# Spreading the operations with sums over a pair of column blocks, and more steps before a turned block is copied, in a hybrid decoder layer on Trainium2

## The chip, the cores and the metric

One core of one Trainium2 chip runs the whole layer. The metric is the device time in microseconds (us); the kernel before was run three times.

## The reference, cut to what matters

The reference is one decoder layer over x of 256 tokens by 2048 features, all in float32:

```
h = rmsnorm(x);  proj = h @ w_in                      # 2048 -> 16400 columns
hm = sigmoid(mo) * head_rmsnorm(mlstm(mq, mk, mv))    # 8 heads
hd = head_rmsnorm(diff_attention(dq, dk, dv))         # 8 heads
y  = sigmoid(gm) * (hm @ w_bm) + sigmoid(gd) * (hd @ w_bd)
x  = x + y @ w_out
h  = rmsnorm(x)
x  = x + (silu(h @ w_gate) * (h @ w_up)) @ w_down     # 2048 -> 5632 -> 2048
out = rmsnorm(x)
```

## The kernel before, in words

**Products.** Each matrix product is cut into column blocks of 512. A `Product` multiplies 256 tokens by one block: 16 steps (`kt`), each with six matmuls (two token halves, and three terms, because activations and weights are each split in a high and a low fp32r part). ScalarE casts the high part of the weights (`wh`, L460 in a `Product`, L313 in a `Pair`), VectorE subtracts it for the low part (`wl`, L461 and L317). One such split covers two steps, is called four units ahead of the matmuls (`AHEAD = 4`), and goes into one of five buffers, so the split for unit u+4 can start when unit u-1 has left TensorE. Raw weights arrive in 1 MB loads on SyncE's queue into `N_RAW = 4` buffers.

**Pairs.** In the feed-forward part a `Pair` multiplies one group of input chunks (512 features each) by two column blocks at once: gate and up (`fgu0` to `fgu10`), or two blocks of the down projection (`fd00`, `fd02`, `fd10`, `fd12`, `fd20`). Its first chunk is multiplied in seven operations instead of eight, with sums of blocks (table `SEVEN`): call them s0 to s6. s3 to s6 need a sum of two weight blocks first, an addition on VectorE in place (`sum_up`, L305). Each seven takes 6 matmuls and writes one PSUM bank. The other chunks are plain operations, p0 to p11 for three of them (four to a chunk), each with 12 matmuls into two banks. `Pair.plan` sets the order: one seven, one plain, in turn, and the plain ones that are left at the end: s0 p0 s1 p1 ... s6 p6 p7 ... p11. `fd20` has three chunks, so s0 to s6 and p0 to p7. Eight banks P1 to P8 hold a pair; `quarters` reads them on VectorE (L392) two ticks after each is finished, and the result of a gate-and-up pair is a block `g`.

**Side work.** All other work is written as generators that are resumed by `side.tick()`, so that their instructions stand between those of the products in each engine's program order. A `Product` ticks once a step, a `Pair` once after a seven and twice in a plain one: in both cases once for six matmuls. `yield n` skips n ticks, a bare `yield` none. Generators in one lane run one after the other; the lane `tr` has the transposed copies of y, x1 and g. Where a product needs a chunk whose copy isn't issued yet, `side.until` ticks on the spot until it is.

**Turned blocks.** A block of 256 tokens by 512 features becomes the left operand of the next product when it is transposed. For the kinds named in `TURN` this is `turn_task` (L231): two transposes of 32x32 squares on VectorE (`turned`, L237), one DMA out to DRAM from GpSimd's queue (L242), four DMAs back into `across` (L247), and then, on ScalarE and VectorE, the high and the low part (L260 and L261; with a scale by column first L264, then L265 and L266):

```python
yield 1
...
yield TURN_OUT
t = c4([P, 4, 4 * TT, 32], "across")
for b in range(4):
    nc.gpsimd.dma_start(...)
yield TURN_BACK
hi, lo = dst.alloc(g)
```

With `TURN_OUT, TURN_BACK = 4, 4` the DMA out is issued at the task's 5th tick, the DMAs back at its 10th, the two halves of the copy at its 15th and 16th, and it ends at the 17th (18th where sums are added, `add_up`). GpSimd has no other work there, so it does not wait for ticks: it issues the DMAs back when the DMA out has landed. The kinds not in `TURN` (the last block of y is one) are transposed on TensorE through PSUM (`ps_tr`, L192). An existing helper `turn` (L221) transposes a block without any DMA, in 16 operations on VectorE of 32 partitions each (L227); the convolution's first inputs use it.

**Order around the change.** Products `bd0` to `bd3`, then `wo0` to `wo3`, then `fgu0` to `fgu3`, `fd00`, `fd02`, `fgu4` to `fgu7`, `fd10`, `fd12`, `fgu8` to `fgu10`, `fd20`, and the last two blocks. `bd_done` pushes a block of y, `wo_done` one of x1, and `gate_up_post` one of g, each into lane `tr`. `across_task` chooses the way of transposing.

Of the kernel before, what the change touches and what calls it, by code (L numbers as in the profile page):

```python
# [9 lines left out]
F32 = mybir.dt.float32  # L10
F32R = mybir.dt.float32r
I32 = mybir.dt.int32
AF = mybir.ActivationFunctionType
ALU = mybir.AluOpType
AX = mybir.AxisListType

P = 128
S = 256
# [18 lines left out]
N_T2 = 9  # L37
N_RAW = 4
AHEAD = 4
TURN_OUT, TURN_BACK = 4, 4  # L40
ORDER = (
    "mq0 mk0 mo0 mo1 mv0 mv1 mq1 mk1 mo2 mo3 mv2 mv3 gm0 gm1 gm2 gm3 bm0 bm1 bm2 bm3 "
    "dq0 dk0 dv0 dq1 dk1 dv1 dq2 dk2 dv2 dq3 dk3 dv3 gd0 gd1 gd2 gd3 bd0 bd1 bd2 bd3"
)
N_WARM = (6, 2)
TURN = {"q0", "k0", "hm1", "hm2", "hm3", "dq", "dk", "hd3", "y", "x1", "x1last", "g", "glast4"}


@with_exitstack
def hybrid_block(ctx, tc, x, attn_norm_w, w_in, conv_w, conv_b, b_igate, b_fgate, mlstm_norm_w,  # L50
# [4 lines left out]
    nc = tc.nc  # L55
# [16 lines left out]
    def c4(shape, name, dt=F32):  # L72
        return c4p.tile(shape, dt, tag="c4", name=name)
# [8 lines left out]
    def t2(shape, name, dt=F32):  # L82
        return smp.tile(shape, dt, tag="t2", name=name, bufs=N_T2)
# [51 lines left out]
    side = Side()  # L135
# [69 lines left out]
                                               in1=hi[:, k].bitcast(F32), op0=ALU.mult, op1=ALU.subtract)  # L205

    def across_task(kind, tile, dst, g, scale_col=None, rate=2):
        if kind in TURN:
            yield from turn_task(tile, dst, g, scale_col, rate)
        else:  # L210
            yield from transpose_task(lambda tt, j: tile[:, tt, j * P:(j + 1) * P], dst, g, scale_col)

    def transpose_task(src, dst, g, scale_col=None):
        yield 2
        dst.alloc(g)
        transpose_half(src, dst, g, 0, scale_col)
        yield 2
        transpose_half(src, dst, g, 1, scale_col)
        dst.ready[g] = True

    def turn(src, t, rate=2):  # L221

        for n in range(16):
            a, b = n // 4, n % 4
            i = src[32 * a:32 * a + 32].rearrange("p t (k q f) -> p t k q f", q=4, f=32)[:, :, :, b]
            o = t[32 * b:32 * b + 32].rearrange("p k (t q s) -> p t k q s", q=4, s=32)[:, :, :, a]
            nc.vector.transpose(out=o, in_=i)  # L227
            if n % rate == rate - 1:
                yield

    def turn_task(src, dst, g, scale_col=None, rate=2):  # L231

# [90 lines left out]
    class Pair:  # L323
# [9 lines left out]
        def plan(self, feed):  # L333
            keys, sevens, plain = {}, [], []
            for ch in self.chunks:
                if ch in self.sums:
                    for i, (bank_, (blk, h), add, x) in enumerate(SEVEN):
                        frees = [(ch, 1)] if i == 5 else [(ch, 0)] if i == 6 else []
                        sevens.append((ch, (ch, blk), h, add and ((ch, add[0]), add[1]), [(bank_, x)], frees))
                else:  # L340
                    for blk in range(2):
                        for h in range(2):
                            uses = [((("P1", "P7"), ("P2", "P8"))[blk][t], (t, h)) for t in range(TT)]
                            plain.append((ch, (ch, blk), h, None, uses, [(ch, blk)] if h else []))
            order = []
            while sevens or plain:
                order += [sevens.pop(0)] if sevens else []
                order += [plain.pop(0)] if plain else []
            self.ops = []
            for ch, raw, h, add, uses, frees in order:  # L350
                if raw not in keys:
                    keys[raw] = len(feed.groups)
                    feed.groups.append((self, raw))
                self.ops.append(Op(self, ch, keys[raw], h, add and (keys[add[0]], add[1]), uses,
                                   [keys[f] for f in frees]))
            feed.units += self.ops
            names = [b for op in self.ops for b, _ in op.uses]
            self.left = {b: 2 * names.count(b) for b in names}
# [30 lines left out]
    def quarters(pair):  # L389

        def op(o, i0, i1, op_):
            nc.vector.tensor_tensor(out=o, in0=i0, in1=i1, op=op_)  # L392
        ps = pair.banks
        yield from pair.after("P3", 2)
        s3, u, v, x = (t2([P, 512], f"q{i}") for i in range(4))
        nc.scalar.copy(out=s3, in_=ps["P3"])
        yield from pair.after("P6", 2)
        op(u, s3, ps["P6"], ALU.subtract)
        op(v, u, ps["P4"], ALU.add)
        yield  # L400
        op(x, v, ps["P5"], ALU.subtract)
        op(u, ps["P5"], u, ALU.subtract)
        for t, c, b, o, op_ in ((0, 0, "P1", s3, ALU.add), (1, 0, "P7", v, ALU.subtract),
                                (0, 1, "P2", u, ALU.add), (1, 1, "P8", x, ALU.add)):
            yield from pair.after(b, 2)
            op(o, ps[b], o, op_)
            yield t, c, o
# [190 lines left out]
    def warm_up(n):  # L598

        wps = accp.tile([P, 512], F32, tag="acc", name="ps_warm")  # L600
        for _ in range(n):
            nc.tensor.matmul(wps[:, 0:P], lhsT=wz, rhs=wz, start=True, stop=True)
# [21 lines left out]
    def start_hook(kt):  # L624
        def f():
            c, j = kt // 4, kt % 4
            if kt < 2:
                xt_half(0, kt, 1)
                if kt == 0:
                    warm_up(N_WARM[1])  # L630
            if c < 3 and j >= 2:
# [133 lines left out]
    def conv_task(tok, ft0, dst):  # L765
# [3 lines left out]
        dst.alloc(0)  # L769
        if dst.name in TURN:  # L770
            t = c4([P, 4, S], "turned")
            yield from turn(tok, t)
        for pr in range(2):
            y = t2([P, 2, S], "cv")
            if dst.name in TURN:
                ps = t[:, 2 * pr:2 * pr + 2]
# [85 lines left out]
    def mlstm_group(g, q, k, va):  # L862
        while not (gt and q.ready[0] and k.ready[0]):
            yield
        hraw = c4([P, TT, 2, DV], "hraw")
        ssq = small([P, 4], "ssq")
        ts = []
        for j in range(2):
            ts.append(side.spawn(mlstm_head(2 * g + j, 2 * (g % 2) + j, q, k, va, j, hraw, ssq)))
            yield 3  # L870
        while not (all(t[2] for t in ts) and g in so):
            yield
        yield 1
        rs = norm_pair(ssq, "m")
        yield 1
        for tt in range(TT):
            for j in range(2):
                nc.vector.scalar_tensor_tensor(out=hraw[:, tt, j], in0=hraw[:, tt, j],
                                               scalar=rs[:, 2 * tt + j:2 * tt + j + 1],
                                               in1=so[g][:, tt, j * DV:(j + 1) * DV],  # L880
                                               op0=ALU.mult, op1=ALU.mult)
            yield
        del so[g]
        yield 2
        side.push("across", across_task(f"hm{g}", hraw.rearrange("p t h d -> p t (h d)"), hmT, g, mn_col, 1 if g < 2 else 2))
# [126 lines left out]
    def diff_group(g, q, k, dv):  # L1012
        while not (q.ready[0] and k.ready[0]):
            yield
        hd = c4([P, TT, 2, DV], "hd")
        ssq = small([P, 4], "ssq")
        ts = []
        for j in range(2):
            ts.append(side.spawn(diff_head(j, q, k, dv, hd, ssq)))
            yield 2  # L1020
        while not all(t[2] for t in ts):
            yield
        yield 1
        rs = norm_pair(ssq, "d", 1.0 - LAM_INIT)
        yield 1
        for tt in range(TT):
            for j in range(2):
                nc.vector.tensor_scalar(out=hd[:, tt, j], in0=hd[:, tt, j],
                                        scalar1=rs[:, 2 * tt + j:2 * tt + j + 1], scalar2=None, op0=ALU.mult)
        yield 2  # L1030
        side.push("across", across_task(f"hd{g}", hd.rearrange("p t h d -> p t (h d)"), hdT, g, dn_col))

    def feat_done(side_name):
        def f(acc):
            tok = tokens_of(acc, "dqk")
            dst = Split(1, f"d{side_name}")
            qk[side_name] = dst
            side.push("conv", across_task("d" + side_name, tok, dst, 0, rate=2))
        return f
# [50 lines left out]
    def gate_up_post(gT, i):  # L1090
        def task(pair):
            g = c4([P, TT, 512], "g")
            for got in quarters(pair):
                if got is None:
                    yield
                    continue
                t, c, q = got
                if c == 0:
                    nc.scalar.activation(out=g[:, t], in_=q, func=AF.Silu, scale=r2(t))
                else:  # L1100
                    nc.vector.scalar_tensor_tensor(out=g[:, t], in0=q, scalar=r2(t), in1=g[:, t],
                                                   op0=ALU.mult, op1=ALU.mult)
            side.push("tr", across_task("g", g, gT, i))
        return task

    ss2 = small([P, TT, 4], "ss2", bufs=1)
# [105 lines left out]
    for pi, (f0, f1) in enumerate(parts):  # L1212
        gT = Split(f1 - f0, f"gT{pi}", {0})
# [14 lines left out]

    warm_up(N_WARM[0])

# [66 lines left out]
```

## Time and profile before

| what | us |
|---|---|
| median of three runs | 1810.53 |
| lowest and highest run | 1809.64, 1811.13 |
| the profiled execution, its own time | 1814.74 |
| its span, from the first to the last instruction | 1813.0 |
| TensorE (PE) busy in it | 1746.1 |
| VectorE (DVE) busy | 1262.7 |
| ScalarE (ACT) busy | 911.8 |
| GpSimd (POOL) busy | 88.8 |

Rows are read so: line of the kernel, engine, operation, output tile, inputs, count, then times; "idle before" or "waited for" is time in which the engine had nothing to do, and the name behind it is what ended that wait. A number in the name of an accumulator is left out by the profile, so all pairs of one kind have one name.

### The profile page before, as it was taken

The page shows a single profiled execution, that of the slowest core. Times are in us where ns is not written, and L with a number is a line of the kernel's source. Part 1 is how long each engine was busy: PE and PEld are TensorE (multiplying, and loading weights), DVE is VectorE, ACT ScalarE, POOL GpSimd, SP SyncE. Part 2 cuts the span into 40 slices and gives each one's busy share as a digit, 9 for nine tenths or more (in the row PEclk, how much of TensorE's full clock was granted, in tenths as well). Part 3 has the DMA queues.
Part 4 walks back from the last instruction along what each step waited for, and adds up shares of the span by engine and source line. Part 5 has one row for each costly group of instructions (what it writes and reads, how often), then busy time and mean ns, then how long its engine had stood idle before and what let it go on. Part 6 is the DMA issues. An engine that isn't in the chain of part 4 may idle for free.

```text
span 1813.0 us, 20500 instructions
## 1 busy us (share of the span) xinstructions
PE 1746.1 (96%) x7769; PEld 1432.9 (79%) x7769; DVE 1262.7 (70%) x1678; ACT 911.8 (50%) x1187; POOL 88.8 (5%) x181
## 2 busy tenths in 40 slices
PE   9999999999999999999999998999998999998968
PEld 7888888888888888888888776777886777886756
DVE  6776866655466766764666686777887778886766
ACT  6555655553445555554445554444444444444433
POOL 1000000000010010000101000000000000000000
PEclk9999999999999999999999999999999999999989
DMA  9656575665686676757776565666556666555652
GB/s 306 199 170 186 165 205 169 199 222 191 201 235 189 202 221 197 201 175 219 258 242 221 174 212 183 209 209 209 186 186 203 194 206 209 200 195 186 217 177 93
DMA packets 179955, 363.57 MB, mean 201 GB/s; under 512 B 9984, under 2 KB 11664, under 8 KB 179856
## 3 DMA queue, kind: packets, MB, share of 16 engines
q1 hardware_dynamic: 169744, 330.78, 57.6%
q0 software_dynamic: 10080, 31.47, 5.8%
q8 instruction: 61, 1.00, 0.2%
q14 instruction: 38, 0.31, 0.0%
q10 hardware_dynamic: 32, 0.01, 0.0%
HBM read 344.40 MB, written 17.83 MB: 200 GB/s over the span
## 4 chain that ended last, share of the span: by engine, by line
PE 75%; DVE 8%; DMA 7%; issue 7%; ACT 2%; POOL 1%; ACTq 0%; DVEq 0%; POOLq 0%
DMA across<-across 5%; PE acc_fgu_P L180 3%; PE acc_fgu_P L181 3%; PE acc_fgu_P L179 3%; DVE wl_fgu L317 3%; PE acc_fd_P L180 3%; PE acc_fd_P L179 3%; PE acc_fd_P L181 3%; DMA across<-turned 2%; PE acc_mv L179 2%; PE acc_mo L179 2%; PE acc_dq L179 2%; PE acc_gm L179 2%; PE acc_dk L179 2%; PE acc_gd L179 2%
## 5 line engine op out<-in xcount | busy, mean ns | idle before, releaser
L313 ACT CAST wh_fgu<-wr_fgu 128x1024 fp32r<-128x1024 f32 x209 | 212.0, 1048 | 170.7 <-DVE wr_fgu L305 96.7
L317 DVE TENSOR_TENSOR wl_fgu<-wr_fgu,wh_fgu 128x1024 fp32r<-128x1024 f32 x209 | 250.7, 1219 | 52.9 <-ACT wh_fgu L313 49.9
L180 PE MATMUL acc_fgu_P<-wl_fgu,x1Th 128*128 128x512 f32 x594 | 237.9, 401 | 18.6 <-DVE wl_fgu L317 18.6
L179 PE MATMUL acc_fgu_P<-wh_fgu,x1Th 128*128 128x512 f32 x594 | 236.9, 399 | 18.8 <-ACT wh_fgu L313 17.8
L181 PE MATMUL acc_fgu_P<-wh_fgu,x1Tl 128*128 128x512 f32 x594 | 235.5, 396 | 0.0
L180 PEld LDWEIGHTS acc_fgu_P<-wl_fgu,x1Th 128*128 128x128 f32 x594 | 114.2, 192 | 49.0 <-DVE wl_fgu L317 25.5
L179 PEld LDWEIGHTS acc_fgu_P<-wh_fgu,x1Th 128*128 128x128 f32 x594 | 114.1, 192 | 47.8 <-ACT wh_fgu L313 22.5
L313 ACT CAST wh_fd<-wr_fd 128x1024 fp32r<-128x1024 f32 x91 | 92.3, 1048 | 85.2 <-DVE wr_fd L305 44.2
L181 PEld LDWEIGHTS acc_fgu_P<-wh_fgu,x1Tl 128*128 128x128 f32 x594 | 114.3, 192 | 23.5
L317 DVE TENSOR_TENSOR wl_fd<-wr_fd,wh_fd 128x1024 fp32r<-128x1024 f32 x91 | 108.6, 1219 | 16.6 <-ACT wh_fd L313 15.3
L242 POOL DMA_DIRECT2D across<-turned x30 | 16.9, 565 | 1459.2 <-DVE turned L237 1459.2
L247 POOL DMA_DIRECT2D across<-across x120 | 65.4, 552 | 170.2 <-DMA across<-turned 71.1
L461 DVE TENSOR_TENSOR wl_bm<-wr_bm,wh_bm 128x1024 fp32r<-128x1024 f32 x32 | 39.1, 1225 | 40.6 <-ACT wh_bm L460 40.6
L461 DVE TENSOR_TENSOR wl_bd<-wr_bd,wh_bd 128x1024 fp32r<-128x1024 f32 x32 | 39.1, 1224 | 33.4 <-ACT wh_bd L460 33.4
L461 DVE TENSOR_TENSOR wl_dv<-wr_dv,wh_dv 128x1024 fp32r<-128x1024 f32 x32 | 38.9, 1219 | 33.2 <-ACT wh_dv L460 33.2
L461 DVE TENSOR_TENSOR wl_gm<-wr_gm,wh_gm 128x1024 fp32r<-128x1024 f32 x32 | 39.1, 1223 | 27.9 <-ACT wh_gm L460 27.7
L461 DVE TENSOR_TENSOR wl_gd<-wr_gd,wh_gd 128x1024 fp32r<-128x1024 f32 x32 | 39.0, 1223 | 27.6 <-ACT wh_gd L460 27.4
L460 ACT CAST wh_bd<-wr_bd 128x1024 fp32r<-128x1024 f32 x32 | 33.7, 1055 | 48.3 <-PE acc_bd L181 40.6
L460 ACT CAST wh_bm<-wr_bm 128x1024 fp32r<-128x1024 f32 x32 | 33.6, 1054 | 47.9 <-PE acc_bm L181 41.1
L461 DVE TENSOR_TENSOR wl_dq<-wr_dq,wh_dq 128x1024 fp32r<-128x1024 f32 x32 | 39.2, 1224 | 26.5 <-ACT wh_dq L460 26.0
L461 DVE TENSOR_TENSOR wl_wo<-wr_wo,wh_wo 128x1024 fp32r<-128x1024 f32 x32 | 38.8, 1220 | 26.2 <-ACT wh_wo L460 26.2
L461 DVE TENSOR_TENSOR wl_mv<-wr_mv,wh_mv 128x1024 fp32r<-128x1024 f32 x32 | 38.9, 1221 | 23.1 <-ACT wh_mv L460 22.9
(426 smaller groups left out, 4624.7 us busy)
## 6 DMA issues: line engine op xcount, KB each, us to landing
wr_fgu<-in_w_ffn_gate_dram SPq DMA_DIRECT2D x44, 1024.0 KB, 7.6
wr_fgu<-in_w_ffn_up_dram SPq DMA_DIRECT2D x44, 1024.0 KB, 5.8
wr_fd<-in_w_ffn_down_dram SPq DMA_DIRECT2D x44, 1024.0 KB, 6.0
wr_mo<-in_w_in_dram SPq DMA_DIRECT2D x16, 1024.0 KB, 5.5
wr_mv<-in_w_in_dram SPq DMA_DIRECT2D x16, 1024.0 KB, 5.4
wr_gm<-in_w_in_dram SPq DMA_DIRECT2D x16, 1024.0 KB, 5.6
wr_bm<-in_w_branch_m_dram SPq DMA_DIRECT2D x16, 1024.0 KB, 5.1
wr_dq<-in_w_in_dram SPq DMA_DIRECT2D x16, 1024.0 KB, 5.4
```

The costliest lines, as they stand in the source:

```text
L179: nc.tensor.matmul(o, lhsT=a[0], rhs=b[0], start=first, stop=False)
L180: nc.tensor.matmul(o, lhsT=a[0], rhs=b[1], start=False, stop=False)
L181: nc.tensor.matmul(o, lhsT=a[1], rhs=b[0], start=False, stop=last)
L242: nc.gpsimd.dma_start(out=d.rearrange("a f b n -> (a f) (b n)"), in_=y.rearrange("p b k t s -> p (b k t s)"))
L247: nc.gpsimd.dma_start(out=t[32 * b:32 * b + 32].rearrange("p a u s -> p a (u s)"), in_=d[:, :, b].rearrange("a f n -> f a n"))
L313: nc.scalar.copy(out=hi, in_=r)
L317: nc.vector.tensor_tensor(out=lo, in0=r, in1=hi.bitcast(F32), op=ALU.subtract)
L460: nc.scalar.copy(out=hi[:, i:i + step], in_=r)
L461: nc.vector.tensor_tensor(out=lo[:, i:i + step], in0=r, in1=hi[:, i:i + step].bitcast(F32), op=ALU.subtract)
```

## The change

The order of a pair's operations is no longer alternate: sevens and plain ones are sorted by their relative place, (i + 0.5) / count. For 7 and 12 this gives p0 s0 p1 p2 s1 p3 s2 p4 p5 s3 p6 p7 s4 p8 s5 p9 p10 s6 p11, for 7 and 8 p0 s0 p1 s1 ... p6 s6 p7. `TURN_BACK` goes from 4 to 10, for all that use `turn_task`. The last block of the feed-forward part (`g` of `fgu10`, now kind `glast`) is turned by `turn_short_task`: 16 transposes on VectorE, four to a tick, then the two halves of the copy; no DMA and no trip to DRAM.

```diff
-TURN_OUT, TURN_BACK = 4, 4
+TURN_OUT, TURN_BACK = 4, 10
...
+SHORT = {"glast"}
...
     def across_task(kind, tile, dst, g, scale_col=None, rate=2):
-        if kind in TURN:
+        if kind in SHORT:
+            yield from turn_short_task(tile, dst, g, scale_col, rate)
+        elif kind in TURN:
...
+    def turn_short_task(src, dst, g, scale_col=None, rate=2):
+        yield 1
+        t = c4([P, 4, S], "turned")
+        yield from turn(src, t, rate)
+        hi, lo = dst.alloc(g)
+        for k in range(0, 4, 2):
+            if scale_col is None:
+                nc.scalar.copy(out=hi[:, k:k + 2], in_=t[:, k:k + 2])
+                nc.vector.tensor_tensor(out=lo[:, k:k + 2], in0=t[:, k:k + 2], in1=hi[:, k:k + 2].bitcast(F32),
+                                        op=ALU.subtract)
+            else:
+                for j in (k, k + 1):
+                    sc = scale_col(4 * g + j)
+                    nc.scalar.activation(out=hi[:, j], in_=t[:, j], func=AF.Identity, scale=sc)
+                    nc.vector.scalar_tensor_tensor(out=lo[:, j], in0=t[:, j], scalar=sc, in1=hi[:, j].bitcast(F32),
+                                                   op0=ALU.mult, op1=ALU.subtract)
+            if k == 0:
+                yield
+        yield
+        dst.ready[g] = True
...
-            order = []
-            while sevens or plain:
-                order += [sevens.pop(0)] if sevens else []
-                order += [plain.pop(0)] if plain else []
+
+            order = sorted([((i + 0.5) / len(l), n, x) for n, l in enumerate((sevens, plain)) for i, x in enumerate(l)],
+                           key=lambda t: t[:2])
+            order = [x for _, _, x in order]
...
-            side.push("tr", across_task("g", g, gT, i))
+            side.push("tr", across_task("g" if i < 2 or len(gT.hi) > 3 else "glast", g, gT, i, None, 4))
```

## Rows read from the trace of the kernel before

**Rows 1.** The waits of TensorE, whole span: total us, times, longest.

```profile
PE acc_fgu_P L180 <- DVE wl_fgu L317: 18.6, 16, 2.1
PE acc_fgu_P L179 <- ACT wh_fgu L313: 17.8, 11, 2.6
PE acc_fd_P L179 <- ACT gT2h L260: 14.5, 1, 14.5
```

**Rows 2.** The waits of ScalarE for turned blocks, whole span.

```profile
ACT gT0h L260 <- DMA across<-across: 38.1, 4, 10.1
ACT gT1h L260 <- DMA across<-across: 36.9, 4, 9.5
ACT gT2h L260 <- DMA across<-across: 29.5, 3, 11.1
```

**Rows 3.** Windows, pair by pair: length, each engine's busy us, granted clock, DMA.

```profile
1031.99:1078.76 46.77, 44.42 (x187) 35.81 (x186) 39.47 (x54) 29.16 (x39) 2.74 (x5) 0.96 0.62 202
1078.76:1224.23 145.47, 133.01 (x559) 106.94 (x558) 109.07 (x117) 66.07 (x74) 8.23 (x15) 0.96 0.62 195
1224.23:1271.29 47.06, 44.93 (x187) 35.90 (x186) 37.25 (x40) 21.14 (x23) 2.76 (x5) 0.96 0.61 201
1314.17:1356.33 42.16, 42.16 (x187) 34.91 (x186) 33.47 (x34) 21.10 (x23) 0.00 (x0) 1.00 0.59 200
1356.33:1501.29 144.96, 132.93 (x560) 106.78 (x559) 109.17 (x117) 66.09 (x74) 8.22 (x15) 0.96 0.61 196
1632.51:1730.64 98.13, 88.55 (x374) 71.08 (x372) 73.64 (x80) 44.25 (x50) 5.48 (x10) 0.97 0.63 204
1722.50:1771.00 48.50, 34.02 (x140) 27.45 (x139) 32.13 (x35) 17.34 (x19) 2.74 (x5) 0.82 0.57 179
```

**Rows 4.** Timeline of ScalarE in fgu2: start, length, what, idle before.

```profile
1153.60 0.62 ACT L260 CAST gT0h<-across 128x512 fp32r<-128x512 f32 x1 [8.56 <-DMA across<-across]
```

**Rows 5.** Timeline of GpSimd: DMAs out and back in fgu2, for y2, for x1's last block.

```profile
1136.00 0.56 POOL L242 DMA_DIRECT2D across<-turned  x1 [43.59 <-DVE turned L237]
1142.84 2.19 POOL L247 DMA_DIRECT2D across<-across  x4 [6.29 <-DMA across<-turned]
...
922.30 0.56 POOL L242 DMA_DIRECT2D across<-turned  x1 [15.43 <-DVE turned L237]
925.78 2.18 POOL L247 DMA_DIRECT2D across<-across  x4 [2.92 <-DMA across<-turned]
...
1043.08 0.56 POOL L242 DMA_DIRECT2D across<-turned  x1 [18.10 <-DVE turned L237]
1047.95 2.18 POOL L247 DMA_DIRECT2D across<-across  x4 [4.31 <-issue]
```

**Rows 6.** DMA issues, y2's window (921 to 940), then x1's last (1042 to 1065): median us to landing.

```profile
across<-across POOLq DMA_DIRECT2D x4, 128.0 KB, 4.1
...
across<-across POOLq DMA_DIRECT2D x4, 128.0 KB, 6.0
```

**Rows 7.** TensorE in bd0 to bd3: ns min/median/max, first and last start.

```profile
L179 PE MATMUL acc_bd<-wh_bd,hdTh x128: 389/389/389, 847.6 to 933.9; 128*128 128x512 f32 x128
```

**Rows 8.** VectorE's short transposes; windows: fd20's start, and after its wait.

```profile
L227 DVE STREAM_TRANSPOSE turned<-tok_cv x32: 425/436/441, 39.9 to 126.1; 32x256 f32<-32x256 f32 x32
...
1722.50:1740.30 17.80, 17.80 (x79) 14.43 (x77) 17.12 (x18) 8.94 (x10) 0.56 (x1) 1.00 0.52 170
1754.80:1759.80 5.00, 5.00 (x12) 3.94 (x13) 1.27 (x2) 0.46 (x1) 0.00 (x0) 0.53 0.02 8
```

**Rows 9.** The splits on ScalarE and VectorE, the scaled copy, a window of TensorE's transposes.

```profile
L313 ACT CAST wh_fgu<-wr_fgu 128x1024 fp32r<-128x1024 f32 x209 | 212.0, 1048 | 170.7 <-DVE wr_fgu L305 96.7
...
L317 DVE TENSOR_TENSOR wl_fgu<-wr_fgu,wh_fgu 128x1024 fp32r<-128x1024 f32 x132 | 158.7, 1220 | 36.9 <-ACT wh_fgu L313 34.7
...
L264 ACT ACTIVATE scaled<-across,nw x32: 492/500/512, 270.8 to 1060.0; 128x256 f32<-128x256 f32 x32
...
943.00:952.00 9.00, 1.20 (x8) 0.99 (x8) 1.38 (x2) 1.17 (x2) 1.00 0.59 203
```

## The prediction

> **What bounds the kernel now.** TensorE is busy nearly the whole span, so a change can only win back its waits, and I began with its list of waits [rows 1]. Nearly all lie in the feed-forward pairs: 36.4 us behind the low and high weights, and one wait of 14.5 us for a turned block, gT2h, in `fd20`. Weights late at 36 us could mean that VectorE has too much to do where sevens bunch, which is what the new order would cure. The windows by pair decide this [rows 3]; each stretch runs from a pair's first matmul on sums (s2) to the next pair's. `fgu4`, the fifth stretch, turns no block, has the alternating order, and takes 42.16 us with TensorE busy for all of it; `fgu8` is like it. So the bunching alone costs nothing there. The stretches with a turned block are long: `fgu1` to `fgu3` 145.47, `fgu5` to `fgu7` 144.96, `fgu9` and `fgu10` 98.13, eight pairs in 388.56 us, where eight times 42.16 is 337.28: 51.3 us over. `fd00`, which turns g3, takes 47.06; `fd10` is like it.
>
> ScalarE's waits say why [rows 2]: eleven times it stands some 9.5 us at the copy of a turned block, since the DMA back has not landed, and the casts of later weights queue behind it. In `fgu2` ScalarE reaches that copy at 1145.0 and starts it at 1153.6 [rows 4]. TensorE lives on the units split ahead, then runs out. The trip is long: DMA out at 1136.0, DMAs back issued at 1142.8, landed at 1153.6, so 17.6 us [rows 5]. The steps leave less: in `bd0` to `bd3` 128 groups of three matmuls start from 847.6 to 933.9 [rows 7], 0.68 us each, so a tick (six matmuls) is 1.36 us, and a copy at the task's 15th tick comes 10 ticks, 13.6 us, after the DMA out at the 5th.
>
> **More steps, where the next need is far.** Six more ticks are 8.2 us: 21.8 us from DMA out to copy, against a trip of 17.6. In a gate-and-up pair (31 ticks) nothing needs the block before the pair after, so the wait of ScalarE should vanish. The new order helps: the additions for s3 and s4, which stood before or between the turning transposes, come after them; each has the size of a split's subtraction, 1.22 us [rows 9], so the DMA out starts some 2.4 us sooner. I take each of the eight pairs to 42.16 plus 0.6: 51.3 - 8 x 0.6 = **-46.5 us** (bounds -20, if the trip grows to where most of a wait is left, and -51).
>
> The 0.6 is a new wait at a pair's start. P7 was last written by p9, now by s6, one unit from the end, and the next pair begins with p0, whose second bank is P7. VectorE's reading of it stands behind the split for the unit four ahead, cast 1.05 and subtraction 1.22 [rows 9]; with some 0.7 of its own it ends 3 us after s6. TensorE gets there after p11 and three matmuls, 2.7 + 0.7 = 3.4 us. The margin is thin. Also both raw buffers of chunk 0 are now held through most of a pair, leaving two of four for the stream. `fgu4`, `fgu8`, `fd02` and `fd12` pay the same without a gain: **+2.4** (0 to +6).
>
> **fgu0.** 46.77 now, 4.6 over [rows 3]; the even order takes its burst away: **-4.0** (0 to -4.6), before the two waits below.
>
> **fd00 and fd10.** Chunk 3 (g3) is needed by p8, formerly after 23 ticks, now after 21. The task starts at the pair's 2nd tick, so its copy would come at the 22nd: `side.until` issues it on the spot, 28.6 us into the pair. The DMA out is at the 6th, 8.2 us, with about 1 us of lateness on VectorE, so the block lands at 9.2 + 17.6 = 27, just in time; but the copy now stands before TensorE: a cast of 1.05 for the current split, 0.62 for the high part [rows 4, 9], some 0.7 for the low: 2.4, and about 1.9 for a lower clock after it. `fd00` is 4.9 over now; after, 2.4 + 1.9 + 0.6 = 4.9; `fd10` I take as the same: **0** for both (-8 to +10).
>
> **fd20, no DMA.** Here g10 is needed after 13 ticks, and the trip cost the 14.5 us. The last stretch [rows 3], from its first matmul to its last, is 48.50 us; 138 matmuls at 0.227 are 31.3, so 17.2 over. After the wait twelve matmuls took 5.0 us at a granted clock of 0.53, about the lower level of 1.2 GHz, where they would take 2.7 at the upper one [rows 7, 8]: after 14.5 us of standing still the clock cost 2.3 us more. I add some 2 us to each long wait. Now 16 transposes of 0.436 us [rows 8] are 7.0 us of VectorE, where it was busy 17.12 of 17.80 us before the need [rows 8]. p4 now comes after 12 ticks, 16.3 us. If nothing else moved, VectorE would be 17.1 + 7.0 - 16.3 = 7.8 us late; as sums that came early come later, it may be none. I take 3.9, plus 1.7 for the clock, plus 0.6: 6.2 left, **-11 us** (-6 to -16).
>
> The Trainium skill (VectorE: DVE Perf Modes, Rules for kernel authors) advises TensorE for a full 128x128 transpose whose result may lie in PSUM, and VectorE for squares of 32. That speaks against this way: the trace's eight such transposes of y's last block took TensorE 1.20 us [rows 9], so by the rule this part would give some 15 us instead of 11 and the sum come out 4 us lower. The sum goes by the route that the change takes.
>
> **More steps, where the next need is near.** This is what the change costs. A task of the lane `tr` now lasts 23 ticks, not 17, and a `Product` 16; so the lane falls behind.
>
> *y.* From the end of `bd0` (847.6 and 16 x 1.36, 869.4) y0 runs in ticks 1 to 23, y1 24 to 46, y2 from 47 on: its DMA out is at tick 51, formerly 39 (869.4 + 39 x 1.36 = 922.4; the trace has 922.3 [rows 5], so the count holds). `wo0` needs it after tick 56, 5 ticks or 6.8 us later. The trip was 3.5 to the DMAs back, 1.6 to the issue of the last of them, 4.1 to landing [rows 5, 6]: 9.2 us; x1's last block took 4.9 + 1.6 + 6.0 = 12.5. TensorE waits 9.2 - 6.8 + 1 for the copy = 3.4, or 6.7 by the longer trip; I take 4.8, 2 for the clock, and 1.7 because y's last block, queued behind, is turned right before its use: **+8.5** (+5 to +13). It was hidden under `bd3` and `wo0`.
>
> *x1, block 2.* It now starts at tick 48, where `fgu0` starts, DMA out at 52; p4 needs it after 59. 7 ticks are 9.5 us; VectorE's queue adds about 1. The trip of x1's last block was 12.5 us, in the loaded pairs 17.6. Scaled copy to the first use: 2 x 0.5 [rows 9] + 0.62 = 1.6. Wait: 12.5 + 1 + 1.6 - 9.5 = 5.6; I take 6 and 2 for the clock: **+8** (+4 to +13).
>
> *x1, last block.* It starts when block 2 is done, at the stalled p4; DMA out at its 5th tick, p8's need after its 10th: 6.8 us. Wait: 12.5 + 1 + 1.6 - 6.8 = 8.3, up to 13 with the longer trip, less what the half clock already gives: 8, and 2 for the clock: **+10** (+5 to +14). Formerly 16 ticks lay between. More steps don't help in these places: `until` cuts them short; the delay comes from the tasks before.
>
> *Elsewhere free.* The copies of hm, dq, dk and hd come 8 us later, and hd's last block another 8 through dk before it. They are hidden by the products between: hm's and hd's last block are needed only in the last quarter of `bm0` and `bd0`, and TensorE waits for none of them now. Without that cover each would cost a wait like y2's, 5 us.
>
> **The sum.** -46.5 + 2.4 - 4 + 0 - 11 + 8.5 + 8 + 10 = -32.6 (all bounds at once: -67 to +30). The profiled execution took 1814.7 us, the median is 1810.5, 4.2 less; so 1782.1 there, and **1778** as a median.
>
> **The rivals.**
> 1. *The lane's delay is hidden*: no waits at y2 and x1. For it: TensorE now waits for no turned block of y or x1. Against it: the counts above, 5 to 7 ticks for trips of 9 to 13 us. It would give 1778 - 26.5 = 1751.5.
> 2. *Slower: the pair boundary.* P7's bank, or the load into one of two free raw buffers, is late at each of some 15 boundaries. From 2.2 us more than the 0.6 taken it eats the whole gain (32.6 / 15), from 2.4 more the kernel is slower by over 0.2%. For it: the 0.4 us margin, and VectorE at 109.07 of 145.47 us [rows 3], which is full where reads bunch. Against it: the DMA share of 0.59 to 0.62 and five units of lead. At 1.4 more it gives 1799, at 3 more 1823.
> 3. *Still too late*: the trip grows in pairs that run faster, so half of the eight pairs' excess stays: 1778 + 23 = 1801. For it: 36.9 and 38.1 us are 9.3 a copy [rows 2], more than the 8.2 added; against it, the earlier DMA out.
>
> **How the numbers follow.** The forecast has 0.60, rival 1 0.13, rival 2 0.15, rival 3 0.12. The forecast's own range is 1762 to 1794, the sum's bounds taken not all at once. To leave out no more than 2 in 10, the range goes to 1753 below (half of rival 1) and 1806 above (most of rivals 2 and 3). A measurement of this kernel tells 0.2%, 3.6 us, from no change. Slower by more: 0.06 of rival 2, 0.02 of rival 3, 0.02 for both together with long waits: 0.10. Within: 0.06. Faster: 0.84.
>
> **What would show it.** ScalarE's waits for gT0h, gT1h and gT2h on DMA near zero, and `fgu1` to `fgu10` at 42 to 43.5 us a pair: right on the steps. New waits of TensorE on yTh or yTl near the middle of `wo0`, and two on x1Th or x1Tl within `fgu0`, 5 to 10 us each: right on the lane. `fd20`'s wait falls to some 4 us, behind gT2h or gT2l. Wrong would be: no wait in `wo0` and `fgu0` (rival 1); waits for a reader of an accumulator (q, L392) or for raw weights at each pair (rival 2); ScalarE still 4 us or more at each copy (rival 3).

## The result, and the profile after

The kernel after takes 1785.26 us (1783.87 to 1786.90 in three runs) against 1810.53: ratio 0.9861, 95% interval 0.9839 to 0.9884, so 1.4% faster. Its profiled execution took 1783.87 us with a span of 1781.8; by the profiled executions the gain is 30.9 us, where the sum said 32.6. The forecast of 1778 is 7.3 us low: 1.7 of it lie in the terms of the sum. The rest is the step from a profiled execution to a median: the one before lay 4.2 above its median, which the forecast took off, and the one after lies 1.4 below its own.

The waits of TensorE in the kernel after (total us, times, longest):

```profile
PE acc_fgu_P L180 <- ACT x1Th L289: 13.3, 2, 7.4
PE acc_wo L180 <- ACT yTh L284: 5.3, 1, 5.3
PE acc_fd_P L180 <- ACT gT2h L241: 5.2, 1, 5.2
PE acc_fgu_P L181 <- DVE wl_fgu L341: 4.1, 3, 1.4
...
PE acc_fd_P L180 <- ACT gT0h L284: 1.7, 1, 1.7
PE acc_fd_P L180 <- ACT gT1h L284: 1.7, 1, 1.7
```

Against [rows 1], the 36.4 us behind weights have become 4.1, and the 14.5 for gT2h 5.2. New are two waits for x1Th in `fgu0` and one for yTh in `wo0`: the lane's delay. The waits of ScalarE for turned blocks in the same kernel:

```profile
ACT gT2h L241 <- DVE turned L230: 9.8, 1, 9.8
ACT scaled L288 <- DMA across<-across: 7.8, 2, 4.7
```

Of the eleven waits for gT0h, gT1h and gT2h on a DMA [rows 2] none is left. The windows by pair of the kernel after (`fgu1`, `fgu2`, `fd00`, `fgu4`; columns as in [rows 3]):

```profile
1109.14:1152.99 43.85, 42.49 (x187) 34.83 (x186) 36.55 (x41) 22.98 (x25) 2.26 (x5) 1.00 0.60 196
1152.99:1195.15 42.16, 42.16 (x187) 34.91 (x186) 37.70 (x40) 22.14 (x24) 3.23 (x6) 1.00 0.71 245
1237.31:1284.15 46.84, 44.53 (x187) 35.75 (x186) 38.37 (x39) 22.38 (x23) 2.20 (x4) 0.96 0.62 200
1326.83:1368.99 42.16, 42.16 (x187) 34.91 (x186) 32.54 (x34) 20.35 (x21) 0.56 (x1) 1.00 0.59 202
```

Five of the eight pairs with a turned block now take 42.16 us, what a pair without one takes, and the other three 43.8. TensorE is busy in all 42.16 us of `fgu2`. What the waits cost besides themselves is seen in the timeline of TensorE after (start, length, what, idle before):

```profile
951.13 0.79 PE L180 MATMUL acc_wo<-wh_wo,yTh 128*128 128x512 f32 x1 [5.34 <-ACT yTh L284]
...
1079.35 0.80 PE L180 MATMUL acc_fgu_P<-wh_fgu,x1Th 128*128 128x512 f32 x1 [7.41 <-ACT x1Th L289]
...
1722.74 0.79 PE L180 MATMUL acc_fd_P<-wh_fd,gT2h 128*128 128x512 f32 x1 [5.24 <-ACT gT2h L241]
...
1726.30 0.39 PE L182 MATMUL acc_fd_P<-wh_fd,gT2l 128*128 128x512 f32 x1
```

From 1722.74 to 1726.30 eight matmuls start, 0.445 us each; the next come 0.23 apart. A wait of 5.2 us therefore costs another 3.56 - 8 x 0.23 = 1.7 us.

By the terms of the sum (us; a pair's stretch is measured as in [rows 3], for `fgu10` to the same place in `fd20` as before):

| term | forecast | measured | from |
|---|---|---|---|
| eight pairs with a turned block | -46.5 | -46.2 | 388.56 to 342.3 |
| `fgu4`, `fgu8`, `fd02`, `fd12` | +2.4 | -0.4 | 42.16, 42.16, 42.68, 42.68 after |
| `fd00` and `fd10` | 0 | -0.9 | 46.84 and 45.54 after |
| `fd20` | -11 | -8.7 | 48.45 to 39.77 |
| y (`bd0` to the end of `wo3`) | +8.5 | +9.2 | 176.2 to 185.4 |
| `fgu0`: even order, x1's block 2 and last | +14 | +15.5 | 46.9 to 62.4 |
| sum (of the unrounded terms) | -32.6 | -31.4 | span: -31.2 |

### The profile page after: what moved, and what is told of

Read it like the earlier page. It is cut to its first block, busy times and chain, and to the rows that moved or that the text cites. A ratio compares the mean times of both kernels' runs of the same rounds, so it can differ in the third digit from the quotient of the medians.

```text
span 1781.8 us, 20497 instructions
## 1 busy us (share of the span) xinstructions
PE 1735.7 (97%) x7769; PEld 1431.4 (80%) x7769; DVE 1272.4 (71%) x1692; ACT 921.1 (52%) x1189; POOL 86.0 (5%) x176
## 4 chain that ended last, share of the span: by engine, by line
PE 91%; DVE 4%; DMA 2%; issue 2%; ACT 2%; POOL 0%; SPq 0%; ACTq 0%; DVEq 0%; POOLq 0%
PE acc_fgu_P L181 7%; PE acc_fgu_P L180 7%; PE acc_fgu_P L182 7%; PE acc_fd_P L180 4%; PE acc_fd_P L182 4%; PE acc_fd_P L181 4%; PE acc_mo L180 2%; PE acc_mv L180 2%; PE acc_gm L180 2%; PE acc_dk L180 2%; PE acc_dq L180 2%; PE acc_gd L180 2%; PE acc_dv L182 2%; PE acc_dv L180 2%; PE acc_gd L182 2%; PE acc_mo L182 2%
## 5 line engine op out<-in xcount | busy, mean ns | idle before, releaser
L180 PE MATMUL acc_fgu_P<-wh_fgu,x1Th 128*128 128x512 f32 x594 | 234.0, 394 | 15.4 <-ACT x1Th L289 13.3
L181 PE MATMUL acc_fgu_P<-wl_fgu,x1Th 128*128 128x512 f32 x594 | 234.0, 394 | 4.1 <-DVE wl_fgu L341 4.1
L180 PEld LDWEIGHTS acc_fgu_P<-wh_fgu,x1Th 128*128 128x128 f32 x594 | 113.0, 190 | 40.3 <-ACT x1Th L289 14.1
L485 DVE TENSOR_TENSOR wl_dk<-wr_dk,wh_dk 128x1024 fp32r<-128x1024 f32 x32 | 39.2, 1224 | 28.7 <-ACT wh_dk L484 28.7
L484 ACT CAST wh_bd<-wr_bd 128x1024 fp32r<-128x1024 f32 x32 | 33.7, 1054 | 47.2 <-PE acc_bd L182 40.5
```

The lines of the kernel that those rows point to most:

```text
L180: nc.tensor.matmul(o, lhsT=a[0], rhs=b[0], start=first, stop=False)
L181: nc.tensor.matmul(o, lhsT=a[0], rhs=b[1], start=False, stop=False)
L484: nc.scalar.copy(out=hi[:, i:i + step], in_=r)
L485: nc.vector.tensor_tensor(out=lo[:, i:i + step], in0=r, in1=hi[:, i:i + step].bitcast(F32), op=ALU.subtract)
```

## The experiments

The theory on record credits the eight pairs to the ten steps; the order adds a DMA out 2.4 us sooner. Its rival: the order does it, and the steps only cost. Ratios below are to the kernel before, timed on the same chip. Its median was 1810.53 to 1814.45 us on the chips used, so the difference of two medians from different chips is uncertain by some 4 us. e10 to e13 add copies of data to DRAM that nothing reads.

**e1: the even order alone**, four steps, g's last block by DRAM:

```diff
+            order = sorted([((i + 0.5) / len(l), n, x) for n, l in enumerate((sevens, plain)) for i, x in enumerate(l)],
+                           key=lambda t: t[:2])
+            order = [x for _, _, x in order]
```

> Only the even order, on the kernel before. Theory A (ScalarE standing before the DMA back makes the weights late): the copy still comes ten ticks after the DMA out, but the DMA out starts some 1 to 3 us sooner in a pair, so ScalarE still stands 6 to 8 us at each copy of g instead of 9.5, and the eight pairs with a turned block lose only part of their 51 us: total 1790 to 1803 us, no waits for y, and for x1 at most 2 us. Theory B (bunched sums make the weights late): nearly all of the gain in the pairs comes from the order, 1765 to 1772 us.

Measured: 1755.88 against 1814.45, ratio 0.9681 [0.9666, 0.9695]. This is 29 us faster than the whole change (33 us when each is taken from the kernel before on its own chip), and below both ranges expected. Windows of e1, `fgu2` and `fd00`; then its waits of ScalarE, and its waits of TensorE:

```profile
1126.81:1168.97 42.16, 42.16 (x187) 34.91 (x186) 37.40 (x40) 21.93 (x24) 3.13 (x6) 1.00 0.73 243
...
1211.13:1253.81 42.68, 42.68 (x187) 34.92 (x186) 37.27 (x40) 21.99 (x23) 2.20 (x4) 1.00 0.67 221
```

```profile
ACT gT0h L260 <- DMA across<-across: 10.6, 4, 5.3
```

```profile
PE acc_fd_P L179 <- ACT gT2h L260: 12.3, 1, 12.3
PE acc_fgu_P L179 <- ACT x1Th L265: 2.9, 1, 2.9
PE acc_fgu_P L180 <- DVE wl_fgu L317: 1.3, 2, 0.9
```

With ten ticks between DMA out and copy, as before, the pairs are cured: ScalarE's waits for gT0h fall from 38.1 [rows 2] to 10.6, and 5.3 of that is `fd00`. `fd00` and `fd10` fall to 42.68 each, which the whole change does not reach. A sooner DMA out does little of this: counted from the pair's first matmul it comes 1.1 to 1.4 us sooner in seven of the eleven pairs that turn a block of g, but 0.8 to 2.1 us later in `fgu2`, `fgu6` and `fgu10` (`fgu2`: 13.4 us, 12.7 before). What changes is the trip, from the DMA out to the landing of the last DMA back: in `fgu2` out at 1126.6 and copy at 1138.0, 11.4 us, against 17.6 before; over the eleven blocks 10.6 to 15.2 us (median 11.9), against 17.5 to 18.8 (median 18.4). ScalarE comes to the copy 9.8 us after the DMA out and waits 1.57 us, where before it came after 9.0 us and waited 8.56 [rows 4, 5]:

```profile
1138.03 0.62 ACT L260 CAST gT0h<-across 128x512 fp32r<-128x512 f32 x1 [1.57 <-DMA across<-across]
```

So the trip still does not fit between the two; what is left of the wait is covered by the units split ahead. Two views of that stretch in the kernel before, its window and SyncE's issues:

```profile
1136.00:1153.60 17.60, 17.60 (x79) 14.57 (x78) 10.16 (x9) 5.12 (x6) 2.74 (x5) 1.00 0.97 293
```

```profile
1135.11 0.37 SPq L433 DMA_DIRECT2D wr_fgu<-in_w_ffn_up_dram  x1
1138.00 0.37 SPq L433 DMA_DIRECT2D wr_fgu<-in_w_ffn_gate_dram  x1
1142.66 0.37 SPq L433 DMA_DIRECT2D wr_fgu<-in_w_ffn_up_dram  x1
1143.95 2.74 SPq L433 DMA_DIRECT2D wr_fgu<-in_w_ffn_gate_dram  x2
```

And the same two in e1:

```profile
1126.60:1138.00 11.40, 11.40 (x52) 9.45 (x51) 11.25 (x10) 5.06 (x5) 2.74 (x5) 1.00 0.93 296
```

```profile
1124.03 0.37 SPq L433 DMA_DIRECT2D wr_fgu<-in_w_ffn_up_dram  x1
1129.75 0.37 SPq L433 DMA_DIRECT2D wr_fgu<-in_w_ffn_gate_dram  x1
1134.44 0.37 SPq L433 DMA_DIRECT2D wr_fgu<-in_w_ffn_up_dram  x1
1136.90 0.37 SPq L433 DMA_DIRECT2D wr_fgu<-in_w_ffn_gate_dram  x1
```

Before, five weight loads of 1 MB are issued in 12 us, from just ahead of the trip on; with the even order four in 13 us, the last when the trip is nearly over. The rate is the same (293 and 296 GB/s, the last number of a window), so the bytes that pass, 5.2 and 3.4 MB, follow from the two lengths and explain neither. VectorE's load does not explain them: it is busy for 10.16 of 17.60 us in the long trip and for 11.25 of 11.40 us in the short one. Nor does GpSimd's issue of the four DMAs back, 2.19 us [rows 5] and 2.18. The DMAs themselves take longer to land (before, then e1; median us from issue to landing):

```profile
across<-turned POOLq DMA_DIRECT2D x1, 512.0 KB, 6.6
across<-across POOLq DMA_DIRECT2D x4, 128.0 KB, 8.7
...
across<-turned POOLq DMA_DIRECT2D x1, 512.0 KB, 3.9
across<-across POOLq DMA_DIRECT2D x4, 128.0 KB, 5.4
```

That points at the loads beside the trip. e8 to e13 try to test it, and e12 bears it out.

**e2: ten steps alone**, in the old order:

```diff
-TURN_OUT, TURN_BACK = 4, 4
+TURN_OUT, TURN_BACK = 4, 10
```

> Only the ten steps, on the kernel before. Theory A: ScalarE's waits at the copies of g nearly vanish and the eight pairs lose 40 to 46 of their 51 us; the waits for y2 and for two blocks of x1 come as in the changed kernel, in fgu0 some 3 us shorter each since the alternating order needs chunks 2 and 3 two ticks later (+19 to +23 in all); fd20 keeps its wait of 14.5 us: 1785 to 1793 us. Theory B: the pairs stay as they were and only the lane's waits are added, 1829 to 1834 us.

Measured: 1788.99 against 1814.45, ratio 0.9867 [0.9851, 0.9884]. The eight pairs fall to 42.2 to 43.1 here too, with the trip still long: in `fgu2` the DMA out is at 1152.05 and the last DMA back lands 17.5 us later; ScalarE comes to the copy at 1170.23, 18.2 us after the DMA out, and does not wait for it. The order, with its bunched sums, is the old one here, so theory B is out. The steps do what the prediction says, and bring its costs. Of the two waits for x1, which were to be some 3 us shorter each than in the whole change, one is 1.7 us shorter (4.1) and the other 2.6 us longer (10.0). Waits of TensorE in e2:

```profile
PE acc_fd_P L179 <- ACT gT2h L260: 15.3, 1, 15.3
PE acc_fgu_P L179 <- ACT x1Th L265: 14.1, 2, 10.0
PE acc_wo L179 <- ACT yTh L260: 5.6, 1, 5.6
```

Order and steps cover the same wait. Each removes it alone (-49.4 us over the eight pairs in e1, -49.5 in e2); together they remove it once (-46.2).

**e3: the last block's short way alone** (`turn_short_task` and kind `glast`, old order, four steps).

> Only the last block of g without a DMA, on the kernel before, old order and four steps. Both theories: fd20's wait of 14.5 us falls to 5 to 8 us, set by VectorE's 16 transposes, and nothing else moves: 1801 to 1805 us. If the wait came from the trip alone and VectorE had room, it would fall to 1 us or less: 1795.

Measured: 1803.73 against 1814.45, ratio 0.9939 [0.9923, 0.9956]: 10.7 us. The time is as expected, the wait is not: for gT2h it falls from 14.5 to 1.1, where 5 to 8 were expected, and those for wl_fd, which were to stay, rise from 2.8 (three) to 6.8 (six). The transposes stand on VectorE among the subtractions for these low weights. In the old order p4 of `fd20` stands after 13 ticks, in the even one after 12. The short way takes `fd20` from 48.45 to 37.94 us here, but only from 46.36 to 41.02 in the even order (e1 against e7).

**e7: the change with four steps.**

```diff
-TURN_OUT, TURN_BACK = 4, 10
+TURN_OUT, TURN_BACK = 4, 4
```

> The changed kernel with four steps everywhere: order and the short way for the last block, without the longer steps. If the steps only cost beside the order, it keeps the 42 us pairs, loses all waits for y and x1 and the forced copies in fd00 and fd10: 1745 to 1751 us, 35 to 39 below the changed kernel. If the steps still gain in some pairs, 1755 to 1765.

Measured: 1750.04 against 1812.04, ratio 0.9643 [0.9617, 0.9668]. The waits for yTh, gT0h and gT1h are gone and x1Th's falls from 13.3 to 2.4. The ten steps cost the change 35 us (37 when each is taken from the kernel before on its own chip).

**e4: the change with four steps for y and x1 alone**; g keeps ten.

```diff
+NEAR = {"y": 4, "x1": 4, "x1last": 4}
...
-            yield from turn_task(tile, dst, g, scale_col, rate)
+            yield from turn_task(tile, dst, g, scale_col, rate, NEAR.get(kind, TURN_BACK))
```

> The changed kernel, but blocks of y and x1 keep four steps before the copy. Theory A (the lane's longer tasks make y2 and two blocks of x1 late): the wait in wo0 goes, of the two in fgu0 at most 2 us stay, some 25 us less than the changed kernel: 1757 to 1764 us. Rival (the waits in fgu0 come from the new order, which needs chunks 2 and 3 of x1 sooner): only the wait in wo0 goes, 1775 to 1778 us.

Measured: 1760.37 against 1814.45, ratio 0.9702 [0.9688, 0.9717]. So some 25 of the 35 us (29 of the 37) are the lane's delay at y and x1, where yTh's wait goes and one of 3.0 us for x1Th stays; the other 8 to 10 lie with the ten steps elsewhere: gT0h and gT1h still wait 1.7 us each in `fd00` and `fd10`, and wl_fgu 4.1.

**e6: even order, four steps, g's last block through TensorE** (kind `glast` without `SHORT`, so through `ps_tr`):

```diff
-            side.push("tr", across_task("g", g, gT, i))
+            side.push("tr", across_task("g" if i < 2 or len(gT.hi) > 3 else "glast", g, gT, i))
```

> The even order with four steps as before, and the last block of g transposed on TensorE through PSUM like y's last block. fd20's wait (12.3 us with the order alone) goes to 0 to 1 us plus 1.2 us of transposes: 1741 to 1747 us. Rival: the two extra PSUM banks must wait for banks that the pair holds, and the wait stays at 5 us or more: 1750.

Measured: 1745.09 (1742.42 to 1747.52) against 1812.04, ratio 0.961 [0.958, 0.964]; the fastest of all, 40 us below the kernel after. Waits of TensorE in e6:

```profile
PE acc_fgu_P L180 <- DVE wl_fgu L317: 3.0, 3, 1.1
PE acc_fgu_P L179 <- ACT x1Th L265: 2.4, 1, 2.4
PE ps_tr L192 <- DVE g L1101: 2.1, 2, 1.1
```

The wait for gT2h (5.2 us in e7) is replaced by 2.1 for the block itself. The median is 5 us below e7's (1748.56 to 1751.87, so the runs do not overlap; the intervals of the two ratios do). The Trainium skill (VectorE: DVE Perf Modes, Rules for kernel authors) advises TensorE for a transpose of a full 128x128 with its result in PSUM; this pair of runs agrees, about 5 us where the prediction had 4.

**e8: the old order, with the turning of a g that isn't needed soon begun 13 ticks later.** The trip meets other loads; steps and order stay (`gend` is added to `TURN`).

```diff
-            yield from turn_task(tile, dst, g, scale_col, rate)
+            yield from turn_task(tile, dst, g, scale_col, rate, 14 if kind == "g" else 1)
...
-        yield 1
+        yield wait
...
-            side.push("tr", across_task("g", g, gT, i))
+            side.push("tr", across_task("g" if i < len(gT.hi) - 1 else "gend", g, gT, i))
```

> The kernel before, but each block of g except the last of a part begins to be turned 13 ticks later in the pair, with the same ten ticks from DMA out to copy. Theory C (the trip is long because the loads of weights bunch in the middle of a pair): later in the pair the trip takes 10 to 13 us instead of 17.6, ScalarE stands 0 to 3 us, the eight pairs lose 30 to 46 us: 1767 to 1784. Theory A (the steps are too few, the trip as long anywhere): ScalarE stands as long as before, 1808 to 1818. Theory B (bunched sums on VectorE): nothing of that bunch is moved, so also no gain.

Measured: 1780.70 against 1812.04, ratio 0.9819 [0.9786, 0.9851]. The window in `fgu2` of e8 from the DMA out to the copy, and ScalarE's waits for gT0h:

```profile
1141.55:1156.13 14.58, 14.58 (x66) 12.05 (x66) 9.16 (x10) 5.55 (x6) 2.74 (x5) 1.00 0.82 255
```

```profile
ACT gT0h L260 <- DMA across<-across: 13.2, 4, 10.6
```

Of four waits for gT0h, 10.6 us are the block of `fgu3`, which is turned in `fd00` at the old time; the other three are 0.5 to 1.1. So with the same order and the same steps the trip in `fgu2` is 3 us shorter at another place in the pair, beside two weight loads instead of five and less traffic (255 GB/s). The larger part of the cure is another: ScalarE comes to the copy 14.1 us after the DMA out there, against 9.0 before, though ten ticks lie between the two in both:

```profile
1156.13 0.62 ACT L260 CAST gT0h<-across 128x512 fp32r<-128x512 f32 x1 [0.53 <-DMA across<-across]
```

The gain is only partial, because `fgu2`, `fgu6` and `fgu10` (47.6, 47.4 and 47.2 us) each have a wait of 2.6 to 3.4 us for low weights some 13 us into the pair, and `fd00` and `fd10` stay at 49.5 and 46.9.

**e9: the raw buffers of chunk 0 freed later** (after p8 and p10 instead of s5 and s6), to move the loads away from the trip in the old order.

```diff
+            for n, blk in ((len(plain) - 4, 1), (len(plain) - 2, 0)):
+                sevens[6 - blk][5].clear()
+                plain[n][5].append((self.chunks[0], blk))
```

> The kernel before with the order and steps as they were; only the two raw buffers of a pair's first chunk are freed, and so the next loads issued, later (at p8 and p10 instead of s5 and s6), which thins the loads out in the middle of a pair. Theory C: the trip falls to 12 to 14 us, ScalarE's wait from 9.5 to 2 to 5 us, the total to 1765 to 1790; fd20's wait shrinks too. Theories A and B: the trip and the waits stay, 1810 to 1818.

Inconclusive: 1813.74 against 1812.04, ratio 0.9994 [0.9972, 1.0015]. The five loads around the trip are issued in the same pattern, and gT0h, gT1h and gT2h wait 36.8, 37.8 and 28.4 us, so the edit did not change what it was to change.

**e10 and e11: e1 with two extra 1 MB copies from the weights to DRAM on SyncE's queue, by program order right behind each g's DMA out; e11 with ten steps for g as well.**

```diff
+        for j in range(extra):
+            x_ = drp.tile([2, P, 1024], F32, tag="extra", name="extra", bufs=4)
+            nc.sync.dma_start(out=x_, in_=w_ffn_up[0].rearrange("(a p) n -> a p n", p=P)[2 * j:2 * j + 2, :, 1024 * g:1024 * g + 1024])
```

> The order alone, four steps, and with each DMA out of a block of g two more copies of 1 MB from weights to DRAM that nothing reads. Theory C (the trip's length is the traffic beside it, at some 295 GB/s): the trip grows by 5 to 7 us, from 11.4 to 16 to 19 us, ScalarE stands 6 to 10 us at each copy, and the pairs get most of their old excess back: 1780 to 1805 us. If the trip's length has another cause (VectorE's load, GpSimd's issue), it stays at 11 to 13 us and the kernel at 1755 to 1762.

> The same extra copies, with ten steps for blocks of g alone. If the steps are a second cover for the same wait, they pay here: pairs near 42.2 to 43 us, the copies in fd00 and fd10 in front of TensorE at 3 to 6 us each, fd20's wait some 5 us longer than with the order alone: 1765 to 1778 us, 15 to 30 below the run with four steps.

Measured: e10 1757.58, ratio 0.9715 [0.969, 0.974]; e11 1766.99, ratio 0.9756 [0.9741, 0.9772]. e10 missed its aim. A copy that waits for nothing is issued as soon as SyncE comes to it: in `fgu2` at 1115.26, 11 us before the DMA out at 1126.06; the trip is 12.6 us there and 10.8 to 15.0 over the eleven blocks, as in e1, and the time is e1's within the intervals. What e11 shows is the price of ten steps for g in the even order: +9.4 us, where 15 to 30 less were expected, with the same 1.7, 1.7 and 4.1 us of waits as e4.

**e12 and e13: the extra copies take the turned block as their source, four of 512 KB, so that they can't run ahead; e13 with ten steps for g.**

```diff
+        for j in range(extra):
+            x_ = drp.tile([P, 4, 256], F32, tag="extra", name="extra", bufs=8)
+            nc.sync.dma_start(out=x_.rearrange("f b n -> f (b n)"), in_=y.rearrange("p b k t s -> p (b k t s)"))
```

> The order alone, four steps, and right behind each DMA out of a block of g, once it is turned, four more copies of that block to DRAM on SyncE's queue (2 MB that nothing reads), so that they run beside the trip and not before it. Theory C: the trip grows by 5 to 7 us to 16 to 19 us, ScalarE stands 7 to 10 us at each copy and the pairs get much of their old excess back: 1785 to 1815 us. If the traffic beside the trip doesn't set its length: 1755 to 1765.

> The same four copies beside each trip, with ten steps for blocks of g alone. If the steps are a second cover for the same wait, they take most of what the four steps lose here: 1765 to 1785 us, ScalarE's waits at the copies of g under 3 us, fd20's wait 16 to 20 us. If the added loss comes from late weights and not from the copies, both runs are alike.

Measured: e12 1832.37 against 1814.04, ratio 1.011 [1.009, 1.013]; e13 1844.09, ratio 1.0174 [1.0157, 1.0191]. SyncE's issues in `fgu2` of e12, then ScalarE's largest wait in it:

```profile
1123.64 0.37 SPq L437 DMA_DIRECT2D wr_fgu<-in_w_ffn_gate_dram  x1
1134.59 2.90 SPq L246 DMA_DIRECT2D extra<-turned  x4
1137.60 1.20 SPq L437 DMA_DIRECT2D wr_fgu<-in_w_ffn_up_dram  x1
```

```profile
ACT wh_fgu L317 <- DMA wr_fgu<-in_w_ffn_up_dram: 80.0, 13, 12.1
```

The loss of 76 us against e1 comes by another mechanism than the one expected: the copies wait at the head of SyncE's queue for the turned block, and the next weight load comes 14 us after the last. ScalarE then waits 80.0 us for raw weights, and only 2.9 for a turned block of g. So ten steps can't help, and e13 is another 12 us slower.

The trip itself, though, did grow as theory C has it. In `fgu2` of e12 the DMA out is at 1134.86, and the last DMA back lands 16.0 us later, where e1 has 11.4. Over the eleven blocks the trip is 15.8 to 17.2 us (median 16.1) in e12 and 15.9 to 17.1 in e13, against 10.6 to 15.2 (median 11.9) in e1, with no more weight loads issued beside it than in e1. The DMAs in `fgu2` of e12 take nearly as long to land as before the change:

```profile
across<-turned POOLq DMA_DIRECT2D x1, 512.0 KB, 5.0
across<-across POOLq DMA_DIRECT2D x4, 128.0 KB, 8.2
```

So 2 MB of added traffic beside the trip lengthens it by some 4 us. It costs ScalarE nothing at the copies but the 2.9 us in `fd20`, since the late raw weights hold ScalarE anyway: in `fgu2` it comes to the copy 18.5 us after the DMA out.

## Why the prediction was right, and the step that was not

**What bounds the kernel now: right.** Bunched sums cost nothing by themselves, the late turned blocks did; e2 shows it, which leaves the order as it was and brings the eight pairs to 42.2 to 43.1 us. One reading there is off: the copy comes not 13.6 us after the DMA out but 9.0 (1145.0 against 1136.0, both in the prediction). The DMA out waits for VectorE's transposes and is at 12.7 us after the pair's first matmul, where its six ticks are 8.2. So the ten steps brought the copy of the eight pairs to 16.2 to 18.2 us after the DMA out, not 21.8; against a trip of 17.6 that is no margin.

**More steps, where the next need is far: the size right, the cause only half.** -46.5 forecast, -46.2 measured. The failed step is "The new order helps: ... so the DMA out starts some 2.4 us sooner". The order helps by itself, fully (e1), and hardly by that: in the kernel after, the DMA out is 1.1 to 1.4 us sooner in seven pairs and 2.5 later in `fgu2`, `fgu6` and `fgu10`. But the trip in the eight pairs lasts 10.6 to 12.7 us instead of 17.6 to 18.8. The prediction took the trip's 17.6 us as fixed when the same diff moves the operations that free the raw buffers, and with them SyncE's loads. The step "The 0.6 is a new wait at a pair's start" failed in its cause too: TensorE waits nowhere for the reader of an accumulator or for raw weights (rival 2 is out), and `fgu4`, `fgu8`, `fd02` and `fd12` give -0.4, not +2.4. What is left over 42.16 is 5.0 us, in the stretches of `fgu1`, `fgu5` and `fgu9`: three waits of 1.4 us for wl_fgu, 12.6 us into the pair behind each, where four operations of VectorE that read out the pair before (2.8 us) stand ahead of the subtraction. e7 has one such wait, of 1.0. That this agrees with the 8 x 0.6 taken is luck.

**fgu0, the even order: not seen.** e1 puts it alone: 47.4 us from the first matmul, against 46.9, where -4.0 was forecast. What the order takes away, a wait of 2.9 us for x1Th brings back:

```profile
1055.39 0.50 PE L179 MATMUL acc_fgu_P<-wh_fgu,x1Th 128*128 128x512 f32 x1 [2.91 <-ACT x1Th L265]
```

It ends 31.7 us into `fgu0`, at p8, which needs x1's last block. p8 stands after 21 ticks of the pair in the even order and after 23 in the old one, so this block is needed 2.7 us sooner. That +14 for the whole of `fgu0` comes so near to the measured +15.5 is in part luck: the -4.0 is missing, and the ten steps add 15.0 us to e1's 47.4, not 18.

**fd00 and fd10: right, 0 against -0.9,** with the forced copies in place (1.7 us of wait each, clock 0.96). That the block lands at 27 us into `fd00`, as counted, is luck: the DMA out is at 11.6 us, not 9.2 (VectorE is 3.4 us late, not 1), and the trip is 15.7 us there, not 17.6. But e1 shows what the ten steps hide here: 42.68 each, together 7 us less.

**fd20, no DMA: the term mis-sized by 2.3 us.** The wait left is 5.2 us instead of 3.9, the clock's part 1.7 as taken, and another wait of 0.8 is for wl_fd. VectorE's rows of the kernel after:

```profile
1711.20 3.57 DVE L230 STREAM_TRANSPOSE turned<-g 32x256 f32<-32x256 f32 x8
...
1716.06 1.78 DVE L230 STREAM_TRANSPOSE turned<-g 32x256 f32<-32x256 f32 x4
...
1720.24 1.79 DVE L230 STREAM_TRANSPOSE turned<-g 32x256 f32<-32x256 f32 x4
```

The 16 transposes take 7.1 us as forecast (0.446 each), but 11 us from first to last: an addition of a sum and two subtractions of splits, 1.22 us each, stand between them. ScalarE waits 9.8 us for them.

**More steps, where the next need is near: right.** y2's DMA out is at 939.84 (922.30 in [rows 5]), x1's last block at 1064.93 (1043.08). On GpSimd in the kernel after:

```profile
939.84 0.56 POOL L266 DMA_DIRECT2D across<-turned  x1 [21.28 <-DVE turned L261]
...
1040.97 0.56 POOL L266 DMA_DIRECT2D across<-turned  x1 [25.38 <-DVE turned L261]
...
1064.93 0.56 POOL L266 DMA_DIRECT2D across<-turned  x1 [15.04 <-DVE turned L261]
```

The counted waits of 4.8, 6 and 8 us came as 5.3, 5.9 and 7.4. Rival 1 is out. e4 and e7 show it by taking it away: some 25 us of the 35 that the ten steps cost.

**Rival 3** is out as well: no wait for a DMA is left at the copies of g, and the trip shrank where it was to grow. Two small slips change nothing: its 9.3 us a copy are 9.4 by [rows 2], and the bounds of the sum, taken all at once, are -66 to +30, not -67.

Why the trip is shorter is shown in the main. Traffic beside it lengthens it: 2 MB added in e12 bring it from a median of 11.9 to 16.1 us. Two weight loads beside it instead of five go with a trip 3 us shorter in the old order (e8), and three or so instead of five with one 6 us shorter in the even order (e1). What stays open is whether the loads are the whole of it, since no run thins out the loads alone; e9 was to do that and did not.

## What to carry to other kernels

Before a wait is bought off with more distance, ask what sets the latency: here a DMA's trip of 17.6 us hung on when the weight loads were issued, and an order that spreads them cures it for nothing, while the distance costs 35 us beside it. A distance in ticks fixes the order of instructions, not the time between them: the same ten ticks were 9.0 us on ScalarE in one place and 14.1 in another (e8), in part because the DMA out, which waits for VectorE, was 4.5 us behind its tick in the one and 1.3 in the other (`fgu1`). A constant of a serial lane is paid by each task in it: count for every user of it what comes next and when that is needed, and set it by user. When a change has several parts, cost each alone and in pairs; two parts that cover the same wait add up to one gain and two costs.

## What the runs showed that was not expected

The time of one round trip of 512 KB each way by DRAM went from 17.6 to 11.4 us in `fgu2`, at nearly the same DMA rate (293 and 296 GB/s), by the order of the operations alone. Loads of the gate's weights landed in 12.1 us (median of four, from 1100 to 1160 us) before, and in 5.2 us in e1 (median of six, from 1090 to 1150).

Four copies of 512 KB that wait for their source on SyncE's queue cost 76 us over eleven blocks, 7 us each, though their issue takes 2.90 us: what counts is what stands behind them.

After a wait of 5.2 us TensorE ran at its lower level of 1.2 GHz: in the window of the eight matmuls behind it in the kernel after, 1722.74 to 1726.30, the granted clock (the third number from the end) is 0.51.

```profile
1722.74:1726.30 3.56, 3.56 (x8) 2.77 (x9) 3.30 (x4) 2.36 (x3) 0.00 (x0) 0.51 0.00 0
```
